# Output projection: where the squares of the last eight products are summed

## The chip, the core and the metric

The kernel runs on one core of a Trainium2 chip. Such a core has five engines that each work through a queue of their own and wait for one another through semaphores: TensorE (PE in the profile: matmuls, with the weight loads as PEld), VectorE (DVE), ScalarE (ACT), GpSimd (POOL), and SyncE (SP), which here only issues transfers between the device memory and the core's on-chip buffers. The on-chip memory is SBUF; matmuls accumulate into PSUM.

The metric is the time of one execution on the device in microseconds (us), as the median of several runs. A profile is one more execution with the hardware profiler on. Its times count from the start of its span.

## The reference, cut to what matters

The model is one layer of a hybrid decoder: two groups of token mixers, an output projection, a squared-ReLU MLP and a gated embedding, over 2048 tokens of width 1024 in float32. The part around the change is this:

```python
mix_out = jnp.einsum('btc,cd->btd', mix, w_out[i])
h = h + rms_norm(mix_out, post_mix_norm[i])
u = jnp.einsum('btd,df->btf', rms_norm(h, pre_mlp_norm[i]), w_mlp_up[i])
y = jnp.einsum('btf,fd->btd', jnp.square(jax.nn.relu(u)), w_mlp_down[i])
```

`rms_norm` divides each token by the root of the mean of its squares over the 1024 columns. So the kernel has to square the output projection's result and sum the squares over all columns of a token before it can normalise.

## The kernel before, in words

Everything is stored transposed: columns of the model lie on the 128 partitions, tokens along the free axis. The 2048 tokens form four quarters `q` of 512, the 1024 columns eight blocks `d` of 128, so a tile is 128x512 in float32. A float32 matmul is made of three matmuls of halves: each operand is split by ScalarE (line 176, a rounded copy) and by VectorE (line 177, the rest: `raw - rounded`), and both halves have to be there before all three matmuls can run.

**The output projection** has 32 products, one for each pair of `q` and `d`, in the order of the list `OUT_ORDER`. Its last eight are 33, 34, 25, 26, 27, 35, 36, 37 (first digit `q`, second `d`). Each product is 24 matmuls into one of four PSUM banks. When it is done, ScalarE copies it to SBUF (line 1504, `yo`), squares it into a tile `sq_o` (line 245), and the square is added to the running sum `acc_o` of its quarter (line 246). Both are in the helper `squares`, whose last argument is the engine that adds; without it this is VectorE. The calls for the MLP's output (`acc_y`) and for the embedding of the last two quarters (`acc_e`) already name GpSimd. The `sq_o` tiles take turns in two buffers, so ScalarE's square of a product needs the sum of an earlier one to be done.

**Beside the last eight products** the same engines prepare the MLP's first block of products, `up(0, 0, ...)`, which follows the last product on TensorE at once. Two things are made:

- `rest_operands` (lines 1366 to 1375) loads tiles of the residual, scales them, forms the sums and differences of a Strassen scheme on VectorE (`b2` to `b6`), and splits each into an operand `t`. It works in four groups `k` from 0 to 3. Line 1375 ends a group: it makes `b6`, from which `t4` is split.
- `two_blocks` and the lines 1478 to 1481 load the first weights of the MLP (`u_raw`), split them, and form their sums and differences. The weights of the first two products are called `11` and `12` (tile `w_u11`), the next two, `22` and `3`, are the halves of the tile `w_u22`. `3` is split from the result of line 1479, which may overwrite its raw tile only after line 1478 has read it, and line 1478 in turn overwrites a tile from which `22` is split.

`up(0, 0, ...)` runs 24 matmuls for `11` and `12`, and then begins `3` and `22`.

**What sets the order:** the code is written in the order of the products. Generators (`later`, `tick`) put in the preparation at counts of eight matmuls. A scheduler then sets the order of each engine's queue. The queues run strictly in order. The instructions on TensorE have the same order before and after the change.

**Behind the last product of a quarter**, `rstd_steps` splits the sum (`hl_o`), lets TensorE sum over the partitions (`nrm_o`) and forms the norm's factor. For quarters 2 and 3, this is used only during the MLP.

Of the kernel before, what the change touches and what calls it, by code (L numbers as in the profile page):

```python
# [96 lines left out]
def trunk(ctx, tc, x, xT, pT, vecs, w_in, w_ab, gdn_a_log, gdn_dt_bias, w_out, w_up, w_down,  # L97
          w_ple, w_gate, consts, out):
    nc = tc.nc
    V, S, G, PE = nc.vector, nc.scalar, nc.gpsimd, nc.tensor  # L100
# [10 lines left out]
    def bank(name, pool=None):  # L111
        return (pool or pm).tile([P, QT], F32, tag="ps", name=name)

    def blk(c):
        return slice(c * P, (c + 1) * P)
# [118 lines left out]
    def squares(acc, src, k, name, eng=V):  # L234

        if acc is None:
            acc = st.tile([P, QT], F32, tag="acc", name=f"acc_{name}", bufs=3)
            S.activation(acc, src, AF.Square)
        else:
            turns[0] += 1  # L240
            if pair[0] and turns[0] % 2:
                sq = st.tile([P, QT], F32, tag="late", name=f"sq_{name}_{k}")
            else:
                sq = st.tile([P, QT], F32, tag="sq", name=f"sq_{name}_{k}", bufs=1)
            S.activation(sq, src, AF.Square)  # L245
            eng.tensor_tensor(acc, acc, sq, ALU.add)  # L246
        return acc
# [19 lines left out]
    def tok(q):  # L267
        return slice(q * QT, (q + 1) * QT)
# [78 lines left out]
    order = [(int(s[0]), int(s[1])) for s in OUT_ORDER.split()]  # L347
# [11 lines left out]
    def ready_at(n):  # L359
        return 0 if n < 3 else sorted(last_use[:n])[n - 3] + 1  # L360

    def stage_at(n):
        return 0 if n < 4 else ready_at(n - 2) + 1

    def stage_out(n):
        staged_out[n] = wp.tile([P, KD, P], F32, tag="raw", name=f"raw_out{n}", bufs=2)
        nc.sync.dma_start(staged_out[n], w_out[tile_of[n]])

    def ready_out(n):
        ready[n] = wp.tile([P, 2, KD, P], F32R, tag="whl", name=f"w_out{n}")  # L370
        split(ready[n], V, staged_out.pop(n))
# [91 lines left out]
    with mixers as mctx:  # L463
# [581 lines left out]
        finished, held_y, square_sums = [], [], {q: None for q in range(NQ)}  # L1045
# [110 lines left out]
        with tc.manual_schedule(engines={mybir.EngineType.SP}):  # L1156
# [5 lines left out]
            for j, (name, key, src, q, h, then, g, b) in enumerate(works):  # L1162
# [3 lines left out]
                ps = bank(f"mm_{name}")  # L1166
# [34 lines left out]
    def later(gen, offsets):  # L1201
        for o in offsets:
            agenda.setdefault(clock[0] + o, []).append(gen)
# [8 lines left out]
    def product(ps, w, xt, start=True, stop=True):  # L1212

        terms = []
        for wk, xk in zip(w, xt):
            terms += [(wk[0], xk[:, 0, :]), (wk[0], xk[:, 1, :]), (wk[1], xk[:, 0, :])]
        n = len(terms)
        for i, (a, b) in enumerate(terms):
            mm(ps, a, b, start and i == 0, stop and i == n - 1)

    def columns(*tiles):

        return [(t[:, 0, k, :], t[:, 1, k, :]) for t in tiles for k in range(t.shape[2])]

    def ytile(name):
        return f2.tile([P, QT], F32, tag="y", name=name, bufs=16)
# [103 lines left out]
    def run(gen):  # L1330
        for _ in gen:
            pass
# [14 lines left out]
    def early_operands():  # L1347

        start_operands(0)
        for k in range(KD // 2):  # L1350
            for n, kk in (("11", k), ("21", k + KD // 2)):
                b = first_b[kk] = ytile(f"be_{kk}")
                nc.sync.dma_start(b, h1d[0][kk])
                V.scalar_tensor_tensor(b, b, col(R_PREMLP + kk), h1_r[0], ALU.mult, ALU.mult)
                moving(0, n, k, b)
                yield

    def rest_operands(rsb):

        held = []  # L1360
        for k in range(KD // 2):
            b11, b21 = first_b[k], first_b[k + KD // 2]
            b12, b22 = ytile(f"b2_0_{k}"), ytile(f"b3_0_{k}")
            for b, kk in ((b12, k), (b22, k + KD // 2)):
                nc.sync.dma_start(b, h1d[1][kk])
                V.scalar_tensor_tensor(b, b, col(R_PREMLP + kk), rsb, ALU.mult, ALU.mult)
            yield
            t3 = ytile(f"b4_0_{k}")
            V.tensor_tensor(t3, b22, b12, ALU.subtract)
            V.tensor_tensor(b12, b12, b11, ALU.subtract)  # L1370
            moving(0, "3", k, t3)
            yield
            t2, t4 = ytile(f"b5_0_{k}"), ytile(f"b6_0_{k}")
            V.tensor_tensor(t2, b22, b12, ALU.subtract)
            V.tensor_tensor(t4, b21, t2, ALU.subtract)
            moving(0, "4", k, t4)
            held.append((t2, b12, b22))
            yield
        for k, raws in enumerate(held):
            for n, raw in zip(("2", "1", "22"), raws):  # L1380
                moving(0, n, k, raw)
                yield
# [43 lines left out]
    def u_block(n, t, raw):  # L1426
        x[n] = t
        split(t.rearrange("p h k n -> p h (k n)"), V, raw)

    def two_blocks(*them):  # L1430

        w = wp.tile([P, 2, KD, P], F32R, tag="whl", name=f"w_u{them[0][0]}")
        halves = [w[:, :, : KD // 2], w[:, :, KD // 2 :]]
        for t, it in zip(halves, them):
            if it:
                u_block(it[0], t, it[1])
        return halves[1]
# [20 lines left out]
    for j, (q, d) in enumerate(order):  # L1458
        if j in finished:
            continue  # L1460
        for n in range(2, len(tile_of)):
            if ready_at(n) == j:
                ready_out(n)
        for n in range(3, len(tile_of)):
            if stage_at(n) == j:
                stage_out(n)
        if j == len(order) - 5:
            u_raw = [wp.tile([P, 2, QT], F32, tag="raw", name=f"u_raw{i}", bufs=2) for i in range(2)]
            a1, a2 = w_up[0], w_up[FF // P // 2]
            for t, i, src in ((u_raw[0], 0, a1[:, : KD // 2]), (u_raw[1], 1, a1[:, KD // 2 :]),  # L1470
                              (u_raw[0], 1, a2[:, : KD // 2]), (u_raw[1], 0, a2[:, KD // 2 :])):
                nc.sync.dma_start(t[:, i].rearrange("p (k n) -> p k n", n=P), src)
        if j == len(order) - 2:
            two_blocks(("11", u_raw[0][:, 0]), ("12", u_raw[1][:, 1]))
        if j == len(order) - 1:
            (a11, a21), (s1, s4) = ((t[:, 0], t[:, 1]) for t in u_raw)
            b22 = two_blocks(("22", s1), None)
            V.tensor_tensor(s1, s1, a21, ALU.add)
            V.tensor_tensor(a21, a11, a21, ALU.subtract)
            V.tensor_tensor(a11, s1, a11, ALU.subtract)  # L1480
            V.tensor_tensor(s4, s4, a11, ALU.subtract)
            u_block("3", b22, a21)
            later(prep, range(3 * KD // 2))
        if early is None and h1_r[0] is not None:
            early = early_operands()
            later(early, range(0, 12, 2))
        if prep is None and h1_r[1] is not None:
            run(early)
            prep = rest_operands(h1_r[1])
            later(prep, range(3 * KD // 2))  # L1490
        if j in held:
            ps = held.pop(j)
        elif order[j] == TOGETHER[0]:
            held = {j + i: bank(f"mmo_{q}_{d}_{i}", pp) for i in range(len(TOGETHER))}
            sides = [columns(ready[load_of[i]]) for i in held]
            for k in range(KD):
                for i, w in zip(held, sides):
                    product(held[i], w[k : k + 1], xin[q][k : k + 1], k == 0, k == KD - 1)
            ps = held.pop(j)
        else:  # L1500
            ps = bank(f"mmo_{q}_{d}", pp)
            product(ps, columns(ready[load_of[j]]), xin[q])
        y = ytile(f"yo{q}_{d}") if q < 2 else tp.tile([P, QT], F32, tag="stg", name=f"yo{q}_{d}")
        S.activation(y, ps, AF.Copy)
        acc = square_sums[q] = squares(square_sums[q], ps, d, f"o{q}")
        made[q][d] = y
        while later_y:
            nc.sync.dma_start(*later_y.pop())
        if q >= 2:
            later_y.append((yod[q][d], y))  # L1510
        if all(of != q for of, _ in order[j + 1 :]) and q < 2:
            later(normed(q, made[q], acc, lambda d, q=q: xT[blk(d), tok(q)], R_POSTMIX, h1d[q], "o", "h"),
                  OUT_LAST if q else OUT_STEPS)
        elif all(of != q for of, _ in order[j + 1 :]):
            later(rstd_steps(acc, 1.0 / D, EPS, f"o{q}", row_of(o_r, q), po, wait=True),
                  (8, 13, 17) if q == 2 else (12, 20, 24))
# [395 lines left out]
    for half in range(2):  # L1912
# [4 lines left out]
        for d in range(KD):  # L1917
# [6 lines left out]
            for s, q in enumerate(qs):  # L1924
# [3 lines left out]
                ps = bank(f"mmg_{q}_{d}", pp)  # L1928
# [60 lines left out]
```

## Time and profile before

| | |
|---|---|
| median of 3 runs | 2638.28 us (2636.36 to 2641.67) |
| the profiled execution, its own time | 2641.29 us |
| span of that execution | 2639.5 us |
| mean granted TensorE clock | 0.999 |
| the last eight products on TensorE | about 1170 to 1214 us |
| first block of the MLP on TensorE | from 1213.87 us |

How to read it: a row of a timeline has the start, the time taken, the engine, the line, the operation, the tiles (output, then inputs, without numbers) and the size; several equal instructions that follow each other are one row with their count. In brackets stands how long the engine was idle just before, and what ended that. An instruction's time overlaps with the next one's: back to back, VectorE starts a 128x512 addition 0.60 us after the one before, though each takes 0.69 us, and the smaller number is its price in a full queue. The page's share of busy time is an average over stages with different limits; what counts here is which wait ends last around 1220 us.

### The profile page before, as it was taken

What the parts mean: (1) busy time and instruction counts of PE and PEld (TensorE: products, weight loads), DVE (VectorE), ACT (ScalarE), POOL (GpSimd) and SP (SyncE); (2) the same over time, 40 slices, a digit from 0 to 9 for tenths busy, and PEclk for the clock granted to TensorE, in tenths of its full rate; (3) what the DMA queues carried; (4) which work ended last, traced back from release to release, by engine and by line L of the source; (5) the groups of instructions that cost most, each with busy time, mean ns of one, the idle gap of its engine ahead of it and who ended that gap; (6) DMA issues with size and microseconds to landing.
All of it is one profiled execution on the core that took longest, in us unless ns stands there. A gap on an engine that the chain in (4) does not pass through costs nothing.

```text
span 2639.5 us, 43913 instructions
## 1 busy us (share of the span) xinstructions
PE 2602.8 (99%) x15593; PEld 2146.0 (81%) x15593; DVE 1965.0 (74%) x4032; ACT 1463.3 (55%) x2991; POOL 137.0 (5%) x147
## 2 busy tenths in 40 slices
PE   8999999999999999999999999999999999999999
PEld 6778788878878888787888888888888888888887
DVE  7778777776777777579988768767877765477775
ACT  7766655465555555566666465555454465565431
POOL 0000000000000000110000000001000001101000
PEclk9999999999999999999999999999999999999999
DMA  8877777767767675764675576665644375677663
GB/s 277 282 258 265 263 256 245 238 222 251 241 213 240 222 237 162 232 203 141 214 236 182 179 233 223 214 211 186 220 150 168 140 245 187 202 252 251 207 223 126
DMA packets 267788, 573.87 MB, mean 217 GB/s; under 512 B 55578, under 2 KB 60152, under 8 KB 250416
## 3 DMA queue, kind: packets, MB, share of 16 engines
q1 hardware_dynamic: 265264, 566.86, 64.5%
q0 software_dynamic: 2304, 4.20, 0.9%
q8 instruction: 123, 2.02, 0.3%
q14 instruction: 97, 0.79, 0.1%
HBM read 410.57 MB, written 160.37 MB: 216 GB/s over the span
## 4 chain that ended last, share of the span: by engine, by line
PE 61%; DMA 2%; issue 2%; DVE 2%; ACT 0%; POOL 0%; SPq 0%; DVEq 0%; POOLq 0%; ACTq 0%
PE d L1210 23%; PE u L1210 23%; PE mmg L1210 7%; PE mm L1176 4%; PE mmo L1059 1%; PE mme L203 1%; DMA yod<-yo 1%; DMA mixT<-mixd 0%; DMA rsb_g<-rd_g 0%; DMA yo<-in_xT_dram 0%; DVE t L177 0%; DMA rd_g<-m_g 0%; DVE acc_o L246 0%; POOL yo L1296 0%; DMA raw_out<-in_w_out_dram 0%
## 5 line engine op out<-in xcount | busy, mean ns | idle before, releaser
L1176 PE MATMUL mm<-xt,w 128*128 128x512 f32 x3072 | 785.5, 401 | 1.6 <-DVE acc_vg L571 0.7
L1176 PEld LDWEIGHTS mm<-xt,w 128*128 128x128 f32 x3072 | 552.8, 188 | 108.3 <-issue 2.1
L1210 PE MATMUL d<-db,da 128*128 128x512 f32 x2688 | 612.8, 389 | 0.0
L1210 PE MATMUL u<-t,wu 128*128 128x512 f32 x2604 | 591.2, 389 | 0.0
L1210 PEld LDWEIGHTS d<-db,da 128*128 128x128 f32 x2688 | 504.5, 188 | 104.8
L1210 PEld LDWEIGHTS u<-t,wu 128*128 128x128 f32 x2604 | 488.7, 188 | 101.5
L230 DVE TENSOR_TENSOR db<-db 128x512 fp32r<-128x512 f32 x224 | 159.5, 712 | 60.0 <-ACT db L229 59.0
L1612 DVE TENSOR_TENSOR u<-u,u 128x512 f32<-128x512 f32 x224 | 150.2, 681 | 52.0 <-PE u L1210 50.4
L229 ACT ACTIVATE db<-db 128x512 fp32r<-128x512 f32 x224 | 140.9, 629 | 67.4 <-DMA db<-hid 63.6
L1210 PE MATMUL mmg<-h2T,wg 128*128 128x512 f32 (+1 forms) x792 | 174.7, 383 | 0.0
L1210 PEld LDWEIGHTS mmg<-h2T,wg 128*128 128x128 f32 x792 | 145.5, 188 | 29.1
L1655 ACT ACTIVATE u<-u 128x512 f32<-128x512 f32 x128 | 80.7, 631 | 152.8 <-DVE u L1612 152.1
L177 DVE TENSOR_TENSOR da<-da 128x512 fp32r<-128x512 f32 x128 | 95.2, 743 | 91.3 <-ACT da L176 89.5
L176 ACT ACTIVATE da<-da 128x512 fp32r<-128x512 f32 x128 | 80.6, 630 | 127.8 <-DMA da<-sumd 100.9
L1210 PE MATMUL mmo<-mixT,w_out 128*128 128x512 f32 x600 | 140.0, 393 | 3.3 <-ACT w_out L176 2.0
L1210 PEld LDWEIGHTS mmo<-mixT,w_out 128*128 128x128 f32 x600 | 113.4, 190 | 28.8 <-DVE w_out L177 2.6
L176 ACT ACTIVATE wu<-a 128x512 fp32r<-128x512 f32 x124 | 75.0, 623 | 55.8 <-DMA a<-in_w_up_dram 52.9
L177 DVE TENSOR_TENSOR wu<-a,wu 128x512 fp32r<-128x512 f32 x124 | 85.9, 694 | 8.3 <-ACT wu L176 8.2
L177 DVE TENSOR_TENSOR da<-dr,da 128x512 fp32r<-128x512 f32 x96 | 68.2, 711 | 23.7 <-ACT da L176 22.2
L1656 ACT ACTIVATE u<-u 128x512 f32<-128x512 f32 x128 | 80.4, 628 | 3.0
L176 ACT ACTIVATE da<-dr 128x512 fp32r<-128x512 f32 x96 | 60.5, 630 | 31.9 <-DMA dr<-in_w_down_dram 21.7
L246 POOL TENSOR_TENSOR acc_y<-acc_y,sq_y 128x512 f32<-128x512 f32 x28 | 37.8, 1351 | 759.5 <-ACT sq_y L245 759.5
(401 smaller groups left out, 3675.4 us busy)
## 6 DMA issues: line engine op xcount, KB each, us to landing
w<-cache_in SPq DMA_DIRECT2D x96, 1024.0 KB
db<-hid SPq DMA_DIRECT2D x224, 256.0 KB
cache_in<-w SPq DMA_DIRECT2D x32, 1024.0 KB
hid<-u SPq DMA_DIRECT2D x128, 256.0 KB
da<-sumd SPq DMA_DIRECT2D x128, 256.0 KB
a<-in_w_up_dram SPq DMA_DIRECT2D x124, 256.0 KB
hid<-ht SPq DMA_DIRECT2D x96, 256.0 KB
dr<-in_w_down_dram SPq DMA_DIRECT2D x96, 256.0 KB
```

What stands on the lines that cost most here:

```text
L176: S.activation(t[:, 0], raw, AF.Copy)
L177: eng.tensor_tensor(t[:, 1], raw, t[:, 0], ALU.subtract)
L203: PE.matmul(ps, a, b, start=i == 0, stop=i == n - 1)
L229: S.activation(t[:, 0], plain(t), AF.Copy)
L230: V.tensor_tensor(t[:, 1], plain(t), t[:, 0], ALU.subtract)
L246: eng.tensor_tensor(acc, acc, sq, ALU.add)
L1059: PE.matmul(ps, w[:, term // 2, k, :], xin[q][k][:, term % 2, :], start=i == 0, stop=i == 3 * KD - 1)
L1176: PE.matmul(ps, *terms[i], start=i == 0, stop=i == nt - 1)
L1210: PE.matmul(ps, a, b, start=start, stop=stop)
L1612: V.tensor_tensor(c[new], c[old], ps, ALU.add)
L1655: S.activation(c[k], c[k], AF.Relu)
L1656: S.activation(c[k], c[k], AF.Square)
```

## The change

For the last eight products, `squares` is called with GpSimd in place of VectorE. Nothing else in the code is changed.

```diff
@@ -1502,7 +1502,7 @@
             product(ps, columns(ready[load_of[j]]), xin[q])
         y = ytile(f"yo{q}_{d}") if q < 2 else tp.tile([P, QT], F32, tag="stg", name=f"yo{q}_{d}")
         S.activation(y, ps, AF.Copy)
-        acc = square_sums[q] = squares(square_sums[q], ps, d, f"o{q}")
+        acc = square_sums[q] = squares(square_sums[q], ps, d, f"o{q}", V if j < len(order) - 8 else G)
         made[q][d] = y
         while later_y:
             nc.sync.dma_start(*later_y.pop())
```

GpSimd's queue, behind the transfers of quarter 1's residual and ahead of the sums of the MLP's output. The names are those above with numbers: `acc_o3` is quarter 3's sum.

```order
 L1296 DMA yo1_7_13494<-in_xT_dram 128x512
+L246 TENSOR_TENSOR acc_o3_13929<-acc_o3_13929,sq_o3_3_14221 128x512
+L246 TENSOR_TENSOR acc_o3_13929<-acc_o3_13929,sq_o3_4_14286 128x512
+L246 TENSOR_TENSOR acc_o2_13834<-acc_o2_13834,sq_o2_5_14339 128x512
+L246 TENSOR_TENSOR acc_o2_13834<-acc_o2_13834,sq_o2_6_14395 128x512
+L246 TENSOR_TENSOR acc_o2_13834<-acc_o2_13834,sq_o2_7_14445 128x512
+L246 TENSOR_TENSOR acc_o3_13929<-acc_o3_13929,sq_o3_5_14476 128x512
+L246 TENSOR_TENSOR acc_o3_13929<-acc_o3_13929,sq_o3_6_14512 128x512
+L246 TENSOR_TENSOR acc_o3_13929<-acc_o3_13929,sq_o3_7_14564 128x512
 L246 TENSOR_TENSOR acc_y0_18289<-acc_y0_18289,sq_y0_2_1_18291 128x512
```

The eight sums are now the only work in GpSimd's queue at that place.

VectorE's queue at the end of the last group of `rest_operands` and the first weights of the MLP (`w_u11` is split in two instructions, first for `11`, then for `12`):

```order
 L1375 TENSOR_TENSOR b6_0_3_14429<-be_7_14234,b5_0_3_14428 128x512
-L246 TENSOR_TENSOR acc_o3_13929<-acc_o3_13929,sq_o3_5_14476 128x512
+L177 TENSOR_TENSOR t4_0_3_14432<-b6_0_3_14429,t4_0_3_14432 128x512
 L177 TENSOR_TENSOR w_u11_14480<-u_raw0_14343,w_u11_14480 128x512
-L177 TENSOR_TENSOR t4_0_3_14432<-b6_0_3_14429,t4_0_3_14432 128x512
 L177 TENSOR_TENSOR w_u11_14480<-u_raw1_14344,w_u11_14480 128x512
 L177 TENSOR_TENSOR t2_0_0_14526<-b5_0_0_14269,t2_0_0_14526 128x512
```

One sum is gone here, and the split of `t4` of group 3 has moved ahead of the split of `11`. Five more sums are gone ahead of this place (those of 33, 34, 25, 26 and 27), one behind it just ahead of the split of `22` (of 36), and one behind the work on `3` (of 37).

ScalarE's queue at the same place:

```order
 L176 ACTIVATE hl_o2_14548<-acc_o2_13834 128x512
 L176 ACTIVATE t3_0_3_14417<-b4_0_3_14414 128x512
+L176 ACTIVATE t4_0_3_14432<-b6_0_3_14429 128x512
 L1504 ACTIVATE yo3_5_14474<-mmo_3_5_14449 128x512
 L245 ACTIVATE sq_o3_5_14476<-mmo_3_5_14449 128x512
 L176 ACTIVATE w_u11_14480<-u_raw0_14343 128x512
-L176 ACTIVATE t4_0_3_14432<-b6_0_3_14429 128x512
 L176 ACTIVATE w_u11_14480<-u_raw1_14344 128x512
 L176 ACTIVATE t2_0_0_14526<-b5_0_0_14269 128x512
```

The split of `t4`, which needs line 1375, now stands ahead of the copy and the square of product 35 and of the split of `11`.

## The prediction

> **What bounds the kernel now.** I read the page's shares first, then the timeline of TensorE around the change, then who ended each wait there, and last the queues of VectorE and ScalarE behind that wait. The page:
>
> ```profile
> span 2639.5 us, 43913 instructions
> PE 2602.8 (99%) x15593; PEld 2146.0 (81%) x15593; DVE 1965.0 (74%) x4032; ACT 1463.3 (55%) x2991; POOL 137.0 (5%) x147
> ```
>
> TensorE is busy 99% of the span, so a change off TensorE gains only what it takes out of TensorE's few waits, and costs only what it puts into one. GpSimd at 5% says nothing yet about whether its time is free. TensorE's timeline where the last product ends and the MLP begins:
>
> ```profile
> 1213.87 5.60 PE L1210 MATMUL u<-t,w_u 128*128 128x512 f32 x24
> 1220.35 0.73 PE L1210 MATMUL u<-t,w_u 128*128 128x512 f32 x2 [0.88 <-ACT w_u L176]
> 1221.49 1.65 PE L1210 MATMUL u<-t,w_u 128*128 128x512 f32 x6 [0.41 <-DVE w_u L177]
> ```
>
> These are the products `11` and `12` (24 matmuls) and then the first matmuls of `3`. With the last matmul of the 24 taking 0.39, the pace is (5.60 - 0.39) / 23 = 0.227 us. The first matmul of `3` was due at 1213.87 + 24 x 0.227 = 1219.3 and the third, which needs VectorE's half of the weight, at 1219.8. They came at 1220.35 and 1221.49. So TensorE loses 1.7 us here, and what ends last is VectorE's split of `3`. VectorE has next to no slack at this place, in a stage of 18 us:
>
> ```profile
> 1205.00:1223.00 18.00, 16.71 (x73) 13.19 (x72) 17.67 (x29) 14.16 (x28) 0.00 (x0) 1.00 0.35 117
> ```
>
> The third pair is VectorE: 17.67 of 18 us busy; GpSimd, the fifth, does nothing. An addition moved off VectorE here looks like a gain of up to 1.7 us. Whether it is one depends on what a GpSimd addition does to VectorE.
>
> **What the change removes.** Eight sums leave VectorE. Its queue before (only the rows used, the first and last of the five sums ahead of line 1375's last row among them):
>
> ```profile
> 1183.26 0.68 DVE L246 TENSOR_TENSOR acc_o<-acc_o,sq_o 128x512 f32<-128x512 f32 x1
> ...
> 1190.48 0.75 DVE L1366 SCALAR_TENSOR_TENSOR b<-b,cols,rn 128x512 f32<-128x512 f32 x1 [0.50 <-DMA b<-h1d]
> ...
> 1205.26 0.69 DVE L246 TENSOR_TENSOR acc_o<-acc_o,sq_o 128x512 f32<-128x512 f32 x1 [0.28 <-ACT sq_o L245]
> ...
> 1210.51 0.69 DVE L1375 TENSOR_TENSOR b<-be,b 128x512 f32<-128x512 f32 x1
> ...
> 1215.94 0.68 DVE L246 TENSOR_TENSOR acc_o<-acc_o,sq_o 128x512 f32<-128x512 f32 x1
> 1216.54 0.68 DVE L177 TENSOR_TENSOR w_u<-u_raw,w_u 128x512 fp32r<-128x512 f32 x1
> ...
> 1218.95 0.68 DVE L1479 TENSOR_TENSOR u_raw<-u_raw 128x512 f32<-128x512 f32 x1
> ...
> 1220.76 0.68 DVE L177 TENSOR_TENSOR w_u<-u_raw,w_u 128x512 fp32r<-128x512 f32 x1
> ```
>
> The last row is the split of `3` that TensorE waits for; `22` is split at 1216.54. A sum takes 1216.54 - 1215.94 = 0.60 us of a full queue. Seven of the eight stand ahead of that split. That of 34 lies just ahead of a wait for a transfer (the row at 1190.48 begins when its data land), so nothing is gained by its removal.
>
> **What it adds: GpSimd's addition holds VectorE up.** The trace has such additions on GpSimd later, in the MLP. Around two of them:
>
> ```profile
> 1788.66 1.29 POOL L246 TENSOR_TENSOR acc_y<-acc_y,sq_y 128x512 f32<-128x512 f32 x1 [0.74 <-ACT sq_y L245]
> 1831.90 1.56 POOL L246 TENSOR_TENSOR acc_y<-acc_y,sq_y 128x512 f32<-128x512 f32 x1 [0.74 <-ACT sq_y L245]
> ```
>
> and VectorE at the same times:
>
> ```profile
> 1788.39 2.47 DVE L1718 TENSOR_TENSOR yu<-yu,d 128x512 f32<-128x512 f32 x4
> ...
> 1831.62 0.68 DVE L1554 TENSOR_TENSOR s<-a,a 128x512 f32<-128x512 f32 x1
> 1832.34 1.67 DVE L1555 TENSOR_TENSOR a<-a,a 128x512 f32<-128x512 f32 x1
> ```
>
> The four additions at 1788.39 read one input from PSUM (`d`); they keep their pace, 2.47 us for four. The addition at 1832.34 has both inputs in SBUF and takes 1.67 us where its neighbour takes 0.68. GpSimd's own addition, begun while that neighbour ran, takes 1.56 instead of 1.29: it ends at 1833.46, 1.16 us after the neighbour's end at 1832.30, and the held instruction ends at 1834.01, 0.55 later. So the two engines take turns whenever VectorE has two inputs in SBUF. [...]
>
> Nearly all that VectorE does between 1180 and 1223 us has both inputs in SBUF. A moved sum therefore gives 0.60 us and takes 0 (where VectorE has nothing to do anyway) to 1.67 - 0.68 = 1.0 us (back to back). I take 1.0 for those in a full queue, as this is the nearer row for a queue without gaps, and 0 for 34.
>
> *Step 1, up to line 1375's last row.* Five sums: gained 4 x 0.60 = 2.4, paid 4 x 1.0 = 4.0. That row comes 1.6 us later. Bounds: -2.4 (nothing held) and 5 x 1.0 - 2.4 = +2.6.
>
> *Step 2, from that row's end to the split of `22` on VectorE.* Before: from 1211.20 to 1216.54, 5.3 us. Now ScalarE's order counts, too:
>
> ```profile
> 1211.24 0.63 ACT L176 ACTIVATE t<-b 128x512 fp32r<-128x512 f32 x1 [0.60 <-DVE b L1375]
> 1211.77 0.61 ACT L176 ACTIVATE w_u<-u_raw 128x512 fp32r<-128x512 f32 x1
> 1212.30 2.18 ACT L176 ACTIVATE t<-b 128x512 fp32r<-128x512 f32 x4
> 1214.38 0.57 ACT L1504 ACTIVATE yo<-mmo 128x512 f32<-128x512 f32 x1
> 1214.86 0.58 ACT L245 ACTIVATE sq_o<-mmo 128x512 f32<-128x512 f32 x1
> 1215.33 0.62 ACT L176 ACTIVATE w_u<-u_raw 128x512 fp32r<-128x512 f32 x1
> ```
>
> The split of `t4` waited 0.60 us for line 1375, and copy, square and the split of `11` were behind ScalarE already. In the new order these three stand behind that wait. From start to start: `t4` 0.53, copy 0.48, square 0.48, `11` and `12` 0.53 each, four `t` 2.08, copy 0.48, and the square of 36 ends 0.58 after its start: 5.7 us after line 1375 the sum of 36 can begin on GpSimd. VectorE is then in the middle of the splits of `t` (0.3 left of one); the sum ends 1.16 after that one, the next split is held and ends 0.55 later, and that of `22` begins 0.08 before this, as back to back: 5.7 + 0.3 + 1.16 + 0.55 - 0.08 = 7.6. That is 2.3 us more than before. Without any holding it would be ScalarE's path alone, 5.7 - 0.1 + 0.62 = 6.2, so 0.9 more: the reordering by itself costs that.
>
> *Step 3, from the split of `22` to that of `3`.* Unchanged, seven instructions of 0.60; the sum of 37 comes behind.
>
> The split of `3` ends 1.6 + 2.3 = 3.9 us later, and TensorE waited for it already, so all 3.9 go to TensorE: some 1.9 as a new wait at 1214 for `11` and 2.0 on top of the 1.7 at 1219. The 1.9: the square of 35 ends 1.6 after line 1375, its sum 1.29 later, VectorE's held split of `11` another 0.55 later, at 1211.2 + 1.6 + 3.4 = 1216.2; TensorE needs it for its third matmul, at 1213.87 + 2 x 0.227 = 1214.3.
>
> *Step 4, the clock.* TensorE's granted clock (the figure behind the busy time) in stretches of 3.41 us:
>
> ```profile
> 17.78:21.19 3.41, 1.72 (x6) 1.00 0.69 160
> 21.19:24.60 3.41, 3.41 (x9) 0.50 0.86 317
> 1219.26:1222.67 3.41, 2.12 (x8) 1.00 0.15 58
> 1222.67:1226.08 3.41, 3.41 (x17) 1.00 0.06 21
> ```
>
> A stretch with 1.72 us of work was followed by one at half clock; one with 2.12, the wait at issue, was not. With 2.0 more, the wait at 1219 leaves less than 1.7 in a stretch unless its border cuts the wait in two. At half clock 3.41 us do the work of 1.7: 1.7 lost. [...]
>
> *Costs of nothing.* The sums on GpSimd are longer and later, but their norm (`hl_o`) is used during the MLP only. The buffers of `sq_o` come back before ScalarE's square after next. On SP's queue the second load of `u_raw0` moves behind two loads of `b` and a store, and a store of product 35 behind three loads: the first is needed by line 1478, just ahead of the row at 1218.95, some 30 us after; the second only frees a buffer for product 37. GpSimd's queue has nothing else there. If all this cover were gone, a transfer would show as VectorE's wait.
>
> **Sum.** 3.9 + 1.7 = +5.6 us on the profiled execution's own 2641.29 us (span 2639.5). Its time lies 3.0 above the median of 2638.28, so the forecast for the median is 2638.28 + 5.6 = 2643.9.
>
> **Rivals.**
> - *A, held, but at full clock:* +3.9, 2642.2. [...] Chance 0.25.
> - *B, held, one stretch at half clock:* +5.6, 2643.9. Chance 0.45, the likeliest.
> - *C, not held, a gain:* the two engines run side by side here, as in the rows at 1788. Step 1 gives -2.4, step 2 +0.9, the wait shrinks by 1.5: 2636.8. It decides if VectorE's rows beside the sums keep to 0.7 us; the row at 1832.34 speaks against it. Chance 0.1.
> - *D, nothing to see:* the sums fall into VectorE's waits for ScalarE, gains and losses cancel: 2638.3. Chance 0.08.
> - *E, worse:* all five held in step 1 (+2.6), and VectorE, 4 us late, lets TensorE wait once more for the weights behind `3`, at the price of one more hold: 2.6 + 2.3 + 1.7 + 1.0 = +7.6, 2645.9. Chance 0.12.
>
> What a measurement of this kernel can tell from no change is about 0.2%, 5.3 us, so the border lies at 2643.6. B lies on it, a bit more than half of it above; E above, and a little of A: 0.45 slower. C gains too little to count as faster; 0.03 is left for that. Range: from between D and A, 2640.0, to E, 2646.2. This leaves out C, D and a little above E.
>
> **What the profile will show.** Steps right: VectorE's rows at lines 177 and 1366 to 1375 of 1.3 to 1.8 us beside eight GpSimd rows of 1.3 to 1.6; line 1375's last row near 1212; TensorE waiting for `w_u` of `11` near 1214 and longer at 1219 to 1225; a stretch with the clock at 0.50 behind it. Wrong: VectorE's rows all at 0.7 (C), no wait for `11` (step 2's order does not matter), or the clock at 1.00 throughout (A). A wait of TensorE after 1230 would be E. A much larger loss would mean that a queue I held for idle was not.

## The result and the profile after

The changed kernel takes 2642.8 us (median of 18 runs, 2640.13 to 2645.64), the kernel before 2638.57 us (18 runs, 2634.13 to 2644.31). The ratio is 1.0019 with a 95% interval of 1.0012 to 1.0025: 5.0 us longer, between 3.2 and 6.6 (the two medians themselves lie 4.2 apart). The forecast was 2643.9 us, 5.6 above a median of 2638.28.

The page gives no hint of it: VectorE has eight instructions less and is busy as long as before (1966.3 us against 1965.0), because of the instructions that are held.

```profile
span 2640.6 us, 43923 instructions
PE 2604.2 (99%) x15593; PEld 2147.9 (81%) x15593; DVE 1966.3 (74%) x4024; ACT 1464.7 (55%) x2991; POOL 153.7 (6%) x155
```

The profiled execution of after took 2642.36 us, only 1.1 more than that of before, though the stage of the change became 5.2 us longer. Single executions differ ahead of this stage: it begins at 1169.99 us before and at 1165.74 after, on unchanged work. What follows the stage is the same again (2639.5 - 1223.43 = 1416.1 us before, 2640.6 - 1224.39 = 1416.2 after). So the runs below are compared by the stage's own length: from TensorE's first matmul behind the norm of quarter 1 to the start of the row of 52 matmuls. Before that was 1223.43 - 1169.99 = 53.44 us. TensorE's timeline after:

```profile
1165.74 22.57 PE L1210 MATMUL mmo<-mixT,w_out 128*128 128x512 f32 x98
1188.54 21.64 PE L1210 MATMUL mmo<-mixT,w_out 128*128 128x512 f32 x94 [0.22 <-DVE w_out L177]
1210.71 0.73 PE L1210 MATMUL u<-t,w_u 128*128 128x512 f32 x2 [0.53 <-ACT w_u L176]
1212.11 5.28 PE L1210 MATMUL u<-t,w_u 128*128 128x512 f32 x22 [0.66 <-DVE w_u L177]
1219.89 0.74 PE L1210 MATMUL u<-t,w_u 128*128 128x512 f32 x2 [2.51 <-ACT w_u L176]
1221.04 2.93 PE L1210 MATMUL u<-t,w_u 128*128 128x512 f32 x6 [0.41 <-DVE w_u L177]
...
1224.39 11.95 PE L1210 MATMUL u<-t,w_u 128*128 128x512 f32 x52
```

The stage is 1224.39 - 1165.74 = 58.65 us, 5.21 more. The row of 94 goes at (21.64 - 0.39) / 93 = 0.2285 us a matmul, so the first of `11` was due at 1188.54 + 94 x 0.2285 = 1210.0 and came at 1210.71; the third was due at 1210.5 and came at 1212.11. That is a new wait of some 1.65 us. The first of `3` was due at 1212.11 + 22 x 0.227 = 1217.1 and came at 1219.89, and the third at 1221.04 instead of 0.45 later: 3.5 us instead of 1.7. Ahead of `11`, a new wait for `w_out` and a few too short to be shown add 0.4: `11` was due 1210.0 - 1165.74 = 44.3 us into the stage, and before it came after 1213.87 - 1169.99 = 43.9. The six matmuls and two of the norm behind it, from 1221.04 to 1224.39, take 3.35 us instead of 1.94 before: most of this ran at half clock. The stretches of 3.41 us around it:

```profile
1111.47:1114.88 3.41, 1.81 (x7) 1.20 (x8) 2.36 (x4) 2.06 (x3) 0.00 (x0) 1.00 1.10 260
1114.88:1118.29 3.41, 3.41 (x10) 2.65 (x9) 0.67 (x2) 1.43 (x3) 0.00 (x0) 0.50 1.08 307
1217.28:1220.69 3.41, 0.84 (x3) 0.30 (x2) 3.41 (x7) 2.06 (x5) 0.00 (x0) 1.00 0.00 0
1220.69:1224.10 3.41, 3.06 (x7) 2.48 (x8) 3.41 (x7) 3.41 (x8) 2.62 (x1) 0.50 0.21 77
```

The first figure behind the length is TensorE's busy time, the one ahead of the DMA share its granted clock. A stretch with 0.84 us of work is followed by one at 0.50. The first two rows are an earlier place of the same execution.

VectorE's timeline, which carries the delay (only the rows used):

```profile
1186.24 1.12 DVE L1366 SCALAR_TENSOR_TENSOR b<-b,cols,rn 128x512 f32<-128x512 f32 x1 [1.11 <-DMA b<-h1d]
...
1191.91 1.66 DVE L1375 TENSOR_TENSOR b<-be,b 128x512 f32<-128x512 f32 x1
...
1207.81 0.69 DVE L1375 TENSOR_TENSOR b<-be,b 128x512 f32<-128x512 f32 x1
...
1210.69 1.96 DVE L177 TENSOR_TENSOR w_u<-u_raw,w_u 128x512 fp32r<-128x512 f32 x2 [0.80 <-ACT w_u L176]
...
1214.99 1.78 DVE L177 TENSOR_TENSOR w_u<-u_raw,w_u 128x512 fp32r<-128x512 f32 x1
1216.69 0.68 DVE L177 TENSOR_TENSOR t<-b,t 128x512 fp32r<-128x512 f32 x1
...
1220.31 0.68 DVE L177 TENSOR_TENSOR w_u<-u_raw,w_u 128x512 fp32r<-128x512 f32 x1
```

and some of GpSimd's eight sums:

```profile
1191.60 1.43 POOL L246 TENSOR_TENSOR acc_o<-acc_o,sq_o 128x512 f32<-128x512 f32 x1 [4.79 <-ACT sq_o L245]
...
1214.37 1.85 POOL L246 TENSOR_TENSOR acc_o<-acc_o,sq_o 128x512 f32<-128x512 f32 x1 [2.87 <-ACT sq_o L245]
1221.48 6.09 POOL L246 TENSOR_TENSOR acc_o<-acc_o,sq_o 128x512 f32<-128x512 f32 x1 [5.25 <-ACT sq_o L245]
```

Beside each of the first seven sums stands a VectorE row of 1.1 to 1.8 us where its like takes 0.69 to 0.75 (1.66 at 1191.91, and 1.78 for the split of `22` at 1214.99). The split of `3`, at 1220.31, is 1220.31 - 1165.74 = 54.57 us into the stage; before it was 1220.76 - 1169.99 = 50.77. So VectorE is 3.80 us late. TensorE pays that (1.65 + 1.8 + 0.4 in the waits above), and 5.21 - 3.80 = 1.4 for the half clock.

In ScalarE's timeline the split of `t4`, now first, waits for line 1375, and copy, square and weights follow behind it:

```profile
1208.54 0.63 ACT L176 ACTIVATE t<-b 128x512 fp32r<-128x512 f32 x1 [2.62 <-DVE b L1375]
1209.08 0.58 ACT L1504 ACTIVATE yo<-mmo 128x512 f32<-128x512 f32 x1
1209.55 0.59 ACT L245 ACTIVATE sq_o<-mmo 128x512 f32<-128x512 f32 x1
1210.03 1.15 ACT L176 ACTIVATE w_u<-u_raw 128x512 fp32r<-128x512 f32 x2
```

### The profile page after: what moved, and what is told of

Read it like the earlier page. It is cut to its first block, busy times and chain, and to the rows that moved or that the text cites. A ratio compares the mean times of both kernels' runs of the same rounds, so it can differ in the third digit from the quotient of the medians.

```text
span 2640.6 us, 43923 instructions
## 1 busy us (share of the span) xinstructions
PE 2604.2 (99%) x15593; PEld 2147.9 (81%) x15593; DVE 1966.3 (74%) x4024; ACT 1464.7 (55%) x2991; POOL 153.7 (6%) x155
## 3 DMA queue, kind: packets, MB, share of 16 engines
q8 instruction: 123, 2.02, 0.3%
## 4 chain that ended last, share of the span: by engine, by line
PE 66%; issue 3%; DVE 3%; DMA 3%; ACT 1%; POOL 0%; SPq 0%; DVEq 0%; POOLq 0%; ACTq 0%
PE d L1210 23%; PE u L1210 23%; PE mm L1176 9%; PE mmg L1210 7%; PE mme L203 1%; PE mmo L1210 1%; DMA yod<-yo 1%; DMA mixT<-mixd 0%; DMA gf_g<-gd 0%; DVE xs_g L748 0%; DVE w_out L177 0%; DVE pr_g L746 0%; DMA yo<-in_xT_dram 0%; DMA rd_h<-m_h 0%; DMA sys_g<-ud_g 0%
```

## The experiments

Three theories stood against each other. H is the prediction's: GpSimd's additions hold VectorE's instructions with two SBUF inputs, and the reordering costs a bit more. O: the reordering on ScalarE costs it all. L: what costs is that GpSimd's sums are longer and land later.

Each profile is read by VectorE's timeline at four points: (a) the start of the line-1366 row that waits for `h1d` (1190.48 before, 1186.24 after), (b) the start of line 1375's last row, (c) the start of the row behind the split of `22`, and (d) that of the split of `3`. In every kernel row (a) waits for its transfer, by 0.5 to 1.2 us, so what VectorE loses or gains ahead of it does not get past it. All figures are us against the kernel before; the ratio is that of total times with its 95% interval.

| kernel | (a) against the stage's start | (a) to (b) | (b) to (c) | (d) against the stage's start | stage | ratio |
|---|---|---|---|---|---|---|
| before | 20.49 | 20.03 | 6.63 | 50.77 | 53.44 | |
| after | +0.01 | +1.54 | +2.25 | +3.80 | +5.21 | 1.0019 (1.0012 to 1.0025) |
| after once more | +0.53 | +1.44 | +2.25 | +4.21 | +5.21 | 1.0015 (1.0007 to 1.0024) |
| narrow sums on VectorE | -2.69 | -1.46 | +0.95 | -3.21 | -2.21 | 1.0005 (0.9996 to 1.0013) |
| GpSimd writes | -0.55 | -1.55 | +1.00 | -1.11 | -1.10 | 0.9996 (0.9986 to 1.0006) |
| both | +0.02 | +2.02 | +0.85 | +2.88 | +4.52 | 1.0030 (1.0018 to 1.0041) |
| two sums deferred | -0.51 | 0.00 | -0.54 | -1.05 | -1.04 | 0.9997 (0.9988 to 1.0007) |
| first five | -1.06 | +1.69 | +1.16 | +1.78 | +3.32 | 1.0012 (1.0001 to 1.0022) |
| last three | -0.25 | +0.01 | +1.18 | +0.93 | +0.97 | 1.0012 (1.0002 to 1.0022) |
| quarters | -0.60 | +1.31 | +1.80 | +3.03 | +4.67 | 1.0017 (1.0008 to 1.0026) |

The column of (a) is the landing of a transfer against TensorE's stage. It differs between executions (by 0.5 us between the two of after), so the effect of an edit is read from the two columns behind it. From (c) to (d) VectorE takes 3.61 to 3.62 us in every row but one: in quarters it takes 4.14, so 0.52 comes on top there.

### The order without GpSimd: narrow sums on VectorE

Here `whole` is a new argument of `squares`, true unless given:

```
-            eng.tensor_tensor(acc, acc, sq, ALU.add)
+            eng.tensor_tensor(acc[:, :QT if whole else 8], acc[:, :QT if whole else 8], sq[:, :QT if whole else 8], ALU.add)
...
-        acc = square_sums[q] = squares(square_sums[q], ps, d, f"o{q}")
+        acc = square_sums[q] = squares(square_sums[q], ps, d, f"o{q}", V, j < len(order) - 8)
```

> The eight sums stay on VectorE, but add 8 of the 512 columns only (the rest of each square is left out of the norm). GpSimd does nothing; ScalarE's and SP's queues are those of the changed kernel, so this is the removal and the reordering without GpSimd. Measured by TensorE's stage, from its first matmul behind the norm of quarter 1 to the start of the row of 52 matmuls: 53.44 us before, 58.65 after. Theory H (VectorE is held up by GpSimd's additions, 1.0 us each; the order costs 0.9): up to line 1375's last row 5 x 0.5 = 2 us sooner, then 0.9 later, so the split of 3 is 1 to 1.5 us sooner and the stage 52.0 to 52.6 us, no half-clock stretch, total time 1 us below before. Theory O (ScalarE's new order is what costs, GpSimd's additions hold nobody): the order is that of after, so the stage stays at 57 to 58.6 us. Theory L (what costs is that GpSimd's sums are longer and land later, not that VectorE is held): as H, 52.0 to 52.6.

TensorE's timeline of this kernel:

```profile
1169.21 43.68 PE L1210 MATMUL mmo<-mixT,w_out 128*128 128x512 f32 x192
1212.73 7.42 PE L1210 MATMUL u<-t,w_u 128*128 128x512 f32 x32
...
1220.44 11.95 PE L1210 MATMUL u<-t,w_u 128*128 128x512 f32 x52
```

No wait is left in the stage: 51.23 us. That is more than expected, since the transfer of (a) landed 2.69 us earlier. By the columns that the edit sets, taking the sums away gains 1.46 us up to line 1375 (2 expected; at 1194.69 VectorE now waits 0.30 us for another transfer), and the reordering costs 0.95 behind it. O needed the reordering alone to cost 5; it falls. And the whole change, had GpSimd held nobody, would have been worth about half a microsecond.

### GpSimd as busy, but writing: nearly all of the square set to zero

```
-            eng.tensor_tensor(acc, acc, sq, ALU.add)
+            _ = whole or G.memset(sq[:, 8:], 0.0), eng.tensor_tensor(acc[:, :QT if whole else 8], acc[:, :QT if whole else 8], sq[:, :QT if whole else 8], ALU.add)
...
-        acc = square_sums[q] = squares(square_sums[q], ps, d, f"o{q}")
+        acc = square_sums[q] = squares(square_sums[q], ps, d, f"o{q}", V if j < len(order) - 8 else G, j < len(order) - 8)
```

> All queues in the order of the changed kernel, GpSimd included, but GpSimd sets 504 columns of the square to zero in SBUF (it writes, and reads nothing) and then adds the other 8 columns, so 504 columns of the eight squares are left out of the norm. GpSimd is about as long at work as with the whole sum, and its results are as late. H: what holds VectorE is GpSimd's reading against VectorE's two SBUF inputs, so next to nothing is held; stage 52 to 53.5 us, VectorE's rows at 0.7 us. If writing holds VectorE as well, rows of 1.3 to 1.8 us stay and the stage is 57 to 59. O and L: 57 to 59 us with VectorE's rows at 0.7 us.

GpSimd's timeline at the square of 35, and its last addition:

```profile
1209.44 0.52 POOL L246 MEMSET sq_o<- 128x504 f32 x1 [5.63 <-ACT sq_o L245]
1209.91 0.20 POOL L246 TENSOR_TENSOR acc_o<-acc_o,sq_o 128x8 f32<-128x8 f32 x1
...
1219.85 4.59 POOL L246 TENSOR_TENSOR acc_o<-acc_o,sq_o 128x8 f32<-128x8 f32 x1
```

GpSimd was at work for 0.7 to 1.1 us a square up to 1215, not quite as long as with the whole sum (1.3). VectorE's rows stay at 0.68 to 0.75 (the largest excess is a pair of 1.52 for 1.41 at 1196.07), the two columns are those of the narrow sums within 0.1, and the stage is 52.34. Writing holds nobody here. Since the sums also land a bit sooner here, L is left to the next run.

### The hold alone: both engines add

```
-            eng.tensor_tensor(acc, acc, sq, ALU.add)
+            _ = (eng or V).tensor_tensor(acc, acc, sq, ALU.add), eng or G.tensor_tensor(sq, sq, sq, ALU.add)
...
-        acc = square_sums[q] = squares(square_sums[q], ps, d, f"o{q}")
+        acc = square_sums[q] = squares(square_sums[q], ps, d, f"o{q}", V if j < len(order) - 8 else None)
```

> Order of the kernel before on every engine; VectorE keeps all its sums, and GpSimd in addition adds each square to itself in place behind it (the norm is not changed). So the hold alone, with nothing removed and nothing reordered on VectorE or ScalarE. H: seven holds of 1.0 us ahead of the split of 3 (five up to line 1375's last row, which comes 5 us later, and two more), so the split of 3 is 5 to 7 us later, stage 58.5 to 60.5 us at full clock and 62 with one stretch at half clock; total 6 to 9 us above before. O: order unchanged, so 53.4 us. L: nobody waits for these results, so 53.4 to 54 us.

TensorE's timeline and GpSimd's last two additions:

```profile
1167.81 22.38 PE L1210 MATMUL mmo<-mixT,w_out 128*128 128x512 f32 x98
...
1221.05 4.07 PE L1210 MATMUL u<-t,w_u 128*128 128x512 f32 x8 [3.41 <-ACT w_u L176]
...
1225.77 12.39 PE L1210 MATMUL u<-t,w_u 128*128 128x512 f32 x52
```

```profile
1211.74 1.42 POOL L246 TENSOR_TENSOR sq_o<-sq_o 128x512 f32<-128x512 f32 x1 [5.15 <-DVE acc_o L246]
1217.40 13.10 POOL L246 TENSOR_TENSOR sq_o<-sq_o 128x512 f32<-128x512 f32 x2 [4.24 <-DVE acc_o L246]
```

Nothing is taken off VectorE, nothing is reordered and nobody in this stage waits for these results, and it is 7.9 us slower in total (4.7 to 10.8). Of that, the profile shows 4.52 in the stage and 0.7 behind it (2642.5 - 1225.77 = 1416.7 us against 1416.1); what more there may be is not explained. That is the hold; it decides for H, and L falls. Its size was below what I expected: VectorE is 2.88 us late at the split of `3`, not 5 to 7, and the stage is 57.96 us, though the clock was at half for two stretches and not one, which is 4.52 - 2.88 = 1.6 us of the stage and the 0.7 behind it:

```profile
1219.76:1223.18 3.42, 2.13 (x4) 1.33 (x5) 3.42 (x6) 2.82 (x6) 3.42 (x1) 0.50 0.09 35
1223.18:1226.59 3.41, 3.41 (x9) 2.63 (x8) 3.41 (x7) 3.41 (x7) 3.41 (x1) 0.50 0.12 44
```

Of seven additions only three cost their full price: their held rows are 1.53 us instead of 0.68 to 0.75, near 0.8 us each. The sum of 33 was lost ahead of (a), that of 34 held a row of 1.08 us, that of 25 fell into a wait for ScalarE. And the addition of 36, begun at 1217.40, was not let in: VectorE ran twelve instructions at its pace of 0.60 us past it, from 1217.85 to 1224.46.

### The parts apart: the first five, the last three

```
-        acc = square_sums[q] = squares(square_sums[q], ps, d, f"o{q}")
+        acc = square_sums[q] = squares(square_sums[q], ps, d, f"o{q}", G if len(order) - 8 <= j < len(order) - 3 else V)
```

> Only the sums of 33, 34, 25, 26 and 27 move to GpSimd (step 1 alone); 35, 36 and 37 stay on VectorE. ScalarE has the splits of t4 ahead of the copy of 35, as in the changed kernel. Nothing is left out. If the terms add up: line 1375's last row 1.7 us later against the norm of quarter 1 (as in the changed kernel), then the reordering, 0.95 us as measured without GpSimd's additions, and up to 0.35 for the two sums that stay, so the split of 3 is 2.6 to 3.0 us later than before, with the wait of TensorE at 3 grown by as much, and the stage 56.1 to 56.5 us at full clock, 57.6 to 58.0 with a stretch at half clock (before 53.44, after 58.65). If instead the loss comes from the last sums alone (the holds at the splits of 11 and 22), the stage stays below 54.5 us.

The second kernel has `G if j >= len(order) - 3 else V` there.

> Only the sums of 35, 36 and 37 move to GpSimd; ScalarE keeps the order of the kernel before at t4. Nothing is left out. If the terms add up: step 1 unchanged; then two sums of 0.60 us less on VectorE and one or two holds of 0.85 to 1.0 us (one where GpSimd's addition is let in late, as in the run with both additions), so the split of 3 between 0.35 us sooner and 0.8 us later, the stage 53.1 to 54.3 us at full clock, up to 55.8 with a stretch at half clock. If the loss comes from the last sums alone, the stage is 57 us or more.

The parts add up. Behind (a), the first five cost 1.69 + 1.16 = 2.85 us (2.6 to 3.0 expected), the last three 0.01 + 1.18 = 1.19 (more than the 0.8 expected), together 4.0, and the whole change 3.79. The total times can't tell the parts apart: the ratio is 1.0012 for both, and the 3.2 us (0.5 to 5.8) that it gives for the last three can't show their 0.97. The stretches of 3.41 us at the wait for `3` show the clock's part, first those of the first five, then those of the last three:

```profile
1211.59:1215.00 3.41, 1.01 (x4) 0.45 (x4) 3.41 (x7) 3.15 (x7) 0.00 (x0) 1.00 0.00 0
1215.00:1218.41 3.41, 3.41 (x9) 2.64 (x10) 3.41 (x7) 3.41 (x8) 0.00 (x0) 0.50 0.22 79
```

```profile
1215.47:1218.88 3.41, 2.30 (x11) 1.56 (x9) 3.41 (x5) 2.89 (x6) 0.68 (x1) 1.00 0.10 35
1218.88:1222.29 3.41, 2.05 (x8) 1.37 (x9) 3.41 (x7) 3.14 (x7) 0.88 (x1) 1.00 0.19 71
```

Both kernels wait as long for `3`, 2.8 to 2.9 us. In the one the wait lies within a stretch, which is left with 1.01 us of work, and the next runs at half clock: the stage is longer by 3.32 where VectorE is late by 1.78, so 1.5 us are the clock's (with one such stretch 57.6 to 58.0 us were expected; the stage is 56.76, as the transfer of (a) landed 1.06 earlier). In the other the clock stays at 1.00 through the wait and behind it: 0.97 longer for 0.93 late. By the author's estimate a border at 1218.88 cuts the wait there, which leaves both stretches over 2.0 us of work; no row shows that border.

### Smaller pieces: each sum cut in four

```
-            eng.tensor_tensor(acc, acc, sq, ALU.add)
+            _ = [eng.tensor_tensor(acc[:, n : n + QT // 4], acc[:, n : n + QT // 4], sq[:, n : n + QT // 4], ALU.add) for n in range(0, QT, QT // 4)] if eng is G and name in ("o2", "o3") else eng.tensor_tensor(acc, acc, sq, ALU.add)
```

> The changed kernel with each of GpSimd's eight sums cut into four additions of 128 columns; the order of all else is unchanged and nothing is left out. If a held VectorE instruction waits until GpSimd's whole instruction is through, a short instruction holds it only about a quarter as long: held rows of 0.9 to 1.1 us instead of 1.66 to 1.78, one to four of them per sum, so the holds cost VectorE 0.3 to 1.0 us a sum instead of 1.0 and the stage is 54.5 to 58 us. If the hold is a sharing of the port at half pace for as long as both have work, the cutting changes nothing: rows of 1.6 to 1.8 us and 58.6 us.

GpSimd's four pieces of the sum of 26, and VectorE beside them:

```profile
1194.38 3.52 POOL L246 TENSOR_TENSOR acc_o<-acc_o,sq_o 128x128 f32<-128x128 f32 x4 [0.63 <-ACT sq_o L245]
```

```profile
1194.23 1.61 DVE L1366 SCALAR_TENSOR_TENSOR b<-b,cols,rn 128x512 f32<-128x512 f32 x2
1195.88 0.83 DVE L1369 TENSOR_TENSOR b<-b,b 128x512 f32<-128x512 f32 x1
1196.74 0.84 DVE L1370 TENSOR_TENSOR b<-b,be 128x512 f32<-128x512 f32 x1
1197.62 0.83 DVE L1374 TENSOR_TENSOR b<-b,b 128x512 f32<-128x512 f32 x1
```

The two engines take turns, instruction by instruction: rows of 0.83 to 0.95 us, some four per sum, instead of one of 1.66 to 1.78. The hold is GpSimd's whole instruction, not a shared pace. In sum it comes to nearly the same, 58.11 us against 58.65, just above the 54.5 to 58 expected: VectorE is 3.03 us late, and the clock was at half for two stretches, from 1218.93 to 1225.76.

### The two sums deferred on VectorE

```
-            later(prep, range(3 * KD // 2))
+            later(prep, range(3 * KD // 2)); [V.scalar_tensor_tensor(a, s, x["3"][:, 1, 0, :1].bitcast(F32), a, ALU.bypass, ALU.add) for a, s in kept]
...
-        acc = square_sums[q] = squares(square_sums[q], ps, d, f"o{q}")
+        acc = square_sums[q] = squares(square_sums[q], ps, d, f"o{q}", kept if j in (len(order) - 3, len(order) - 2) else V)
```

Here `squares` only appends `(acc, sq)` to `kept` for those two.

> The kernel before, with no work on GpSimd, but VectorE's sums of 35 and 36 put behind the split of 3 (each reads a column of that split without using it). Nothing is left out. H says that VectorE's queue sets the wait for 3: two sums of 0.60 us out of it make the split of 3 1.2 us sooner, TensorE's wait there shrinks from 1.7 to 0.5 us, the stage is 52.2 us, and the total 1.2 us below before, unless the square of 37, which now waits for a buffer, holds up something in the MLP. Rival: if TensorE's wait at 3 hangs on ScalarE or a transfer, the stage stays at 53.4 us and the total is the same as before.

VectorE's timeline of this kernel at the split of `22`:

```profile
1213.25 2.49 DVE L177 TENSOR_TENSOR t<-b,t 128x512 fp32r<-128x512 f32 x4
1216.12 0.69 DVE L177 TENSOR_TENSOR w_u<-u_raw,w_u 128x512 fp32r<-128x512 f32 x1 [0.38 <-ACT w_u L176]
```

The stage is 52.40 us, near the 52.2 expected, but half by luck: of the 1.05 us by which the split of `3` is earlier, 0.51 are the transfer's. Without the two sums VectorE waits 0.38 us for ScalarE's half of `22`, so the edit gives 0.54 us instead of 1.2. In the total time nothing is to be seen. With the 51.23 us that the stage took where TensorE never waited (the narrow sums), no placement of these sums can gain more than 2.2 us, less than 0.1% of the kernel.

### The changed kernel once more

> The changed kernel itself once more, to see which of its rows come back: the stage of TensorE 58.65 us within 0.5, its wait for 3 with one stretch at half clock behind it (without it 57.1 us), and GpSimd's sum of 37 let in only 5 us after its start, when VectorE pauses (if that was chance, 1.3 to 1.9 us). Total 4 to 6 us above before.

Its timeline of TensorE, and of GpSimd at the sum of 37:

```profile
1164.24 16.93 PE L1210 MATMUL mmo<-mixT,w_out 128*128 128x512 f32 x74
...
1222.89 11.95 PE L1210 MATMUL u<-t,w_u 128*128 128x512 f32 x52
```

```profile
1220.39 6.08 POOL L246 TENSOR_TENSOR acc_o<-acc_o,sq_o 128x512 f32<-128x512 f32 x1 [5.25 <-ACT sq_o L245]
```

The stage is 58.65 us again, with one half-clock stretch (1218.74 to 1222.15), and the sum of 37 takes 6.08 us again; that was no chance. The total is 4.0 us above before (1.9 to 6.3), at the low end of what was expected.

## Why the prediction was right, and where it was not

**Direction and size.** Right: +5.6 was forecast, the total gave +5.0 (3.2 to 6.6) and the stage +5.21. The ratio of 1.0019 lies just inside the 0.2% that was called the border.

**What the change adds.** Right: the hold is there, and it is the main cause; the reordering is a quarter of VectorE's delay. The kernel in which both engines add shows it with nothing removed, the writing kernel shows it gone. The price of 1.0 us holds where VectorE's queue has work (0.97, 1.03 and 1.03 us for the sums of 25, 26 and 27), but it is the price of a held instruction, not of every sum, and in the kernel where both engines add it was 0.78 to 0.85. That the engines take turns "whenever" VectorE has two inputs in SBUF was too much: the sum of 37 was passed by eight such instructions (below).

**Step 1.** The sum was right (+1.6 forecast, +1.54 measured from (a) to (b)), two of its terms were not. It took four sums ahead of line 1375 for full ones and that of 34 for nothing. But 33 stands ahead of the wait for `h1d` at (a) too: its hold, 1.67 us at line 1251, and its gain were both swallowed there. And 34 was not free: its addition reached past the landing and held the row of 1.12 us by 0.37. So 0.37 + 0.97 + 1.03 + 1.03 = 3.4 was paid, for three sums gained. These gave 0.49, 0.48 and 0.98 instead of 0.60 each: two stood between instructions that without them start 0.72 us apart, not 0.60 (lines 1374 and 1375, at 1191.19 and 1191.91 after; 1.21 apart before, with the sum of 25 between them), and the third had waited 0.28 us for ScalarE. That leaves some 1.5, near the forecast because the errors cancelled; that is luck.

**Step 2.** Right: +2.25 for +2.3 forecast, and 0.95 to 1.0 us for the reordering alone, where 0.9 was forecast; the two kernels without a hold show that part by itself. One detail was not: GpSimd's sum of 36 was to hold the instruction ahead of `22`, with `22` begun 7.6 us after line 1375. It held the split of `22` itself, which began 1214.99 - 1208.50 = 6.5 us after and then took 1.78.

**Step 3.** Right: 3.62 us from (c) to (d) before and after, (d) 3.80 later (forecast 3.9), a new wait of 1.65 for `11` (1.9) and 1.8 on top at `3` (2.0); the other 0.4 went into waits ahead of `11`.

**Step 4.** Right in kind: one stretch at half clock, in both executions of the changed kernel. It cost some 1.4 us instead of 1.7; the stretch was not full of work (3.06 of 3.41 us). Rival A's outcome, held but at full clock, was seen with the last three (0.97 longer for 0.93 late); that a border cut the wait there is the author's estimate. By the total alone A (2642.2) and B (2643.9) can't be told apart, since 2642.8 lies between them; the clock in the rows decides for B.

**The rivals.** C, two engines side by side, falls; where GpSimd only wrote, the gain was there. Its size would have been 0.5 us, not 1.5, since step 1's gain without a hold is 1.46 to 1.55, not 2.4. D and E did not come about: TensorE did not wait again behind `3`. (The range's upper end, 2646.2, is 0.3 above E's own 2645.9; nothing hangs on it.)

**Costs of nothing.** Right. ScalarE waited 1.59 us for the sum of 27 ahead of `hl_o` (at 1204.00), off the path; the loads moved on SP's queue were in time.

## What to carry to other kernels

Moving an elementwise sum with SBUF inputs from a full VectorE to an idle GpSimd was a loss here, where VectorE's own work has two inputs in SBUF: 0.5 to 0.6 us were saved in a full queue and up to 1.0 us paid, since the engines took turns by whole instructions. Count such a price only behind the last wait that swallows delays, and for each stretch of the queue apart: the same sum cost 0, 0.37 or 1.03 us by where it fell. A change of the engine also changes a scheduler's order elsewhere; here that was a quarter of VectorE's delay, and where TensorE's wait left 0.84 us of work in one stretch of 3.41 us, the next ran at a granted clock of 0.50.

## What the runs showed of the hardware that was not expected

**A waiting GpSimd addition was passed for microseconds.** The sum of 37 was issued at 1221.48 and ended at 1227.57, 6.09 us where 1.29 do alone. VectorE's rows beside it, in after:

```profile
1221.51 0.68 DVE L177 TENSOR_TENSOR t<-b,t 128x512 fp32r<-128x512 f32 x1
1222.12 1.28 DVE L177 TENSOR_TENSOR w_u<-u_raw,w_u 128x512 fp32r<-128x512 f32 x2
...
1226.33 0.67 DVE L1612 TENSOR_TENSOR u<-u,u 128x512 f32<-128x512 f32 x1
1226.93 1.19 DVE L177 TENSOR_TENSOR wu<-a,wu 128x512 fp32r<-128x512 f32 x1
```

From 1221.51 on VectorE keeps its 0.60 us pace, and the first instruction that is held is that at 1226.93. The same place gave 6.08 us in two other runs, 4.59 us for an addition of 8 columns, and the additions of 36 and 37 in the kernel with both took 13.10 together. GpSimd's addition began ahead of eight VectorE instructions with two SBUF inputs that went past it. Where it got in can be estimated, with the 1.29 us that it takes alone: 1.29 us before its end is 1226.28, and at 1226.33 VectorE began line 1612, which adds a product from PSUM and so has one SBUF input only. The addition of 8 columns, which takes 0.20 alone, ended at 1224.44, with line 1612 begun at 1224.31. So in these two runs the addition ended 1.24 and 0.13 us behind the start of the first line 1612; that this start let it in was not tested. What lets it in elsewhere between two instructions with two SBUF inputs was not settled.

**The half-clock stretches lay whole multiples of 3.413 us apart.** In after, three of them begin at 19.20, 1114.88 and 1220.69, 321 and 31 x 3.413 us apart, and in before two at 21.19 and 1116.87, 321 x 3.413. Each lasted 3.41 us at a granted clock of 0.50, with 1.00 just ahead of it and just behind it. In after, the stretches of 3.41 us ahead of the last two had 1.81 and 0.84 us of work; with 2.12 us (before, from 1219.26) the next kept the full clock, 1.00. Busy time alone does not settle it: in after, the stretch from 619.94 to 623.35, 145 x 3.413 us ahead of that at 1114.88, had only 1.71 us of work, and the next kept 1.00. Behind half-clock stretches with 2.13 us of work (where both engines add) and 2.86 (quarters) the clock stayed at 0.50, behind one with 3.06 (after) it was 1.00. What counts besides busy time stays open.
